# Prompt scores as two 128-row products with a stack of the keys' high and low halves, in place of a 128-row and a 64-row product

## The chip, the cores and the metric

The kernel runs on one core of one Trainium2 chip. It is one program: one launch reads the inputs from the chip's memory, does one decoder layer and writes all outputs. The metric is the device time of that launch in microseconds (us); lower is better. The figure for the kernel before is the median of three runs.

## The reference

One layer of a hybrid decoder is computed for a prompt of 1024 tokens and for 64 sampled tokens (8 sequences of 8), with a model width of 1024, in float32. Cut to what matters here:

```
mix:  h = rmsnorm(x) * (1 + scale1) + shift1
      ga, gc, xa, qb, kb, vb, qc, kc, vc = split(h @ w_in)
      A: short convolution of 256 channels
      B: 6 heads of width 64, three dilations, combined by their softmax denominators
      C: 6 query heads on 2 key/value heads, window 128, a learned sink for each head
      x = x + gate1 * (concat(A, B, C) @ w_out)
ffn:  x = x + gate2 * (silu(h2 @ w_gate) * (h2 @ w_up)) @ w_down
```

For the prompt's attention every head needs the scores `q . k / 8`, the softmax over the keys that its window (and, in group B, its dilations) allows, and the probabilities' sum of the values.

The products are to keep nearly float32 accuracy while TensorE runs them in float32r, a rounded form. So each operand x is split into two exact float32r halves, `hi = round(x)` and `lo = x - hi`, and `a . b` is taken as `hi.hi + hi.lo + lo.hi`; the product `lo.lo` is left out.

## The kernel before

**Stages.** Tokens lie along the free dimension, features on the 128 partitions. The program first computes the modulation and the first norm, then the input projection and the prompt's attention, then the sampled tokens' attention with the cached keys and values (with the output projection and the first feed-forward blocks of the prompt between its parts), then the feed-forward network. The large products are in `mm3` (L197): for each block of 128 contraction rows three matmuls, L202, L203 and L204, each with its own weights of 128 x 128 and 356 or 366 moving columns. The modulation of later stages is computed in between by `mod_tile` (L170), whose products at L178 use weights of only 32 columns.

**Order.** The code is written as a plain sequence. A scheduler puts each engine's instructions in order when the program is built, by its own estimate of times, and lets work of one stage fill gaps of another. Each engine then runs its list strictly in order and waits on semaphores.

**The prompt's attention** (L453 to L598) runs four times on a pair of heads' keys and values: once for the windowed group C, whose stack serves three query tiles, and three times for group B. The two heads of a block of 128 features lie on partitions 0 to 63 (`hd` = 0) and 64 to 127 (`hd` = 1); `o` is 64 * `hd`.

- `kv_stacks` (L459) prepares the keys. For each head, ScalarE writes the high half of the keys to `KH` on the head's own 64 partitions (L466); a transfer issued by GpSimd copies it to the other 64 partitions (L467); GpSimd subtracts to get the low half `KL`, on the head's own partitions (L468). L475 to L480 transpose the values.
- `attend` (L483) goes through heads and, in each, units of four (group C) or two (group B) blocks of 128 queries. For every two blocks it makes a query tile `QS` of 256 columns: ScalarE writes the high half on the head's 64 partitions (L496), GpSimd the low half on the other 64 (L497). The ring has three such tiles.
- The scores of one block of queries with up to 512 keys take two products into one tile `ps_s` of PSUM (two tiles in the ring). L517 contracts 128 rows, `[q_hi; q_lo] . [k_hi; k_hi]`. L518 contracts the head's 64 rows alone, `q_hi . k_lo`, and adds to it.
- VectorE adds the mask and takes the minimum (L524; the scores carry a minus sign), ScalarE takes the exponential and its sum (L532), VectorE the reciprocal (L534), VectorE or GpSimd the scaling (L535). TensorE transposes the probabilities (L560), ScalarE and VectorE split them (L563, L564), TensorE multiplies by the values (L569, weights of 128 x 128).

There are 48 query tiles (six calls of `attend`, eight tiles in each) and 120 pairs of L517 and L518: 12 pairs have 128 moving columns, 60 have 256, 18 have 384 and 30 have 512.

Of the kernel before, what the change touches and what calls it, by code (L numbers as in the profile page):

```python
# [8 lines left out]
F32 = mybir.dt.float32  # L9
F32R = mybir.dt.float32r  # L10
AF = mybir.ActivationFunctionType
OP = mybir.AluOpType
# [20 lines left out]
# buffers of the rings of tiles  # L33
# [6 lines left out]
# banks of the tags g, s, t, o in PSUM, and the tags that the early products take  # L40
# [4 lines left out]
# VectorE (v) or GpSimd (g) for each chunk; the chunks of the last norm that GpSimd scales  # L45
# [5 lines left out]
# tiles of the modulation after each projection, and gate blocks ahead of the sampled tokens'  # L51
# [12 lines left out]
def _build(nc, tc, d, cst, rows, actp, stream, psum):  # L64
# [18 lines left out]
    def halves(raw, sp=None):  # L83
        """The exact float32r halves of a float32 tile."""
# [35 lines left out]
    # constants  # L120
# [49 lines left out]
    def mod_tile(t, bank="g"):  # L170
        """256 columns of the modulation: a strip of 32 array columns for each quarter of the contraction."""
# [25 lines left out]
    def mm3(ps, sp, kcs, a, n, first=True, last=True):  # L197
        """ps[:, :n] (+)= W^T a for the K chunks, from exact halves of both operands."""
# [15 lines left out]
    def gemm(src, acts, gs, evac):  # L214
        """W^T a of one block of 128 features for the groups gs; src: the two halves of the block."""
# [10 lines left out]
    def inv_rms(pool, sums, n):  # L226
        """1 / sqrt(sums / D + EPS), one Newton step after the table's root."""
# [12 lines left out]
    # ---------------------------------------------------------------- first norm, h  # L240
# [3 lines left out]
    def early_split(b, i):  # L244
        """As split; the float32 tile stays for the product with the shift."""
        wraw[b, i] = load(d["w_in"][b, i], stp, "eraw", 4)
        return halves(wraw[b, i])
# [39 lines left out]
    # The input projection is W^T (x scale) / rms + W^T shift: the shifts are NB more columns of the third group,  # L287
    # except for the first two blocks.
# [21 lines left out]
    # ---------------------------------------------------------------- input projection  # L310
# [3 lines left out]
    def evac_norm(ps, g, r, s, b, scale=None):  # L314
        """The product over the rms of each token; b gets the bias, r the prompt's tokens and s the sampled ones."""
# [42 lines left out]
    def proj_plain(blk, name):  # L358
# [3 lines left out]
        if blk == 2:  # L362
            # the shifts come last
# [46 lines left out]
    def conv_steps(a):  # L410
# [8 lines left out]
        def times(ps, g, t, b, y, ys):  # L419
            """y and ys times the product of the group."""  # L420
# [32 lines left out]
    with tc.tile_pool(name="attn", bufs=1) as at:  # L453
# [4 lines left out]

        def kv_stacks(kn, vn):  # L459
            kr, vr = prow[kn], prow[vn]  # L460
            KH = []
            KL = at.tile([128, SEQ], F32R, tag="KL", bufs=1, name="KL")
            for hd in range(2):
                kh = at.tile([128, SEQ], F32R, tag="KH", bufs=2, name="KH")
                o = 64 * hd
                S.activation(kh[o:o + 64, :], kr[o:o + 64, :SEQ], AF.Copy)  # L466
                G.dma_start(kh[64 - o:128 - o, :], kh[o:o + 64, :])  # L467
                G.tensor_tensor(KL[o:o + 64, :], kr[o:o + 64, :SEQ], kh[o:o + 64, :].bitcast(F32),  # L468
                                op=OP.subtract)
                KH.append(kh)  # L470
# [10 lines left out]
            return KH, KL, Vt  # L481

        def attend(qn, stacks, mixrow, sinks=None):  # L483
            qr = prow[qn]
            KH, KL, Vt = stacks
            windowed = sinks is not None
            U = 4 if windowed else 2
            for hd in range(2):
                o = 64 * hd
                for j in range(8 // U):  # L490
                    P = []
                    for qi in range(U):
                        if qi % 2 == 0:
                            QS = at.tile([128, 256], F32R, tag="QS", bufs=3, name="QS")
                            qsrc = qr[o:o + 64, 128 * (U * j + qi):128 * (U * j + qi) + 256]
                            S.activation(QS[o:o + 64, :], qsrc, AF.Copy)  # L496
                            G.tensor_tensor(QS[64 - o:128 - o, :], qsrc, QS[o:o + 64, :].bitcast(F32),  # L497
                                            op=OP.subtract)
# [14 lines left out]
                        for si, (s0, sn) in enumerate(segs):  # L513
# [3 lines left out]
                            PE.matmul(ps[:, :sn], lhsT=QS[:, qsl], rhs=KH[hd][:, kk], start=True, stop=False)  # L517
                            PE.matmul(ps[:, :sn], lhsT=QS[o:o + 64, qsl], rhs=KL[o:o + 64, kk],  # L518
                                      start=False, stop=True)
# [585 lines left out]
```

## Time and profile before

| what | us |
|---|---|
| median of the three runs | 1460.31 |
| lowest and highest of them | 1457.1, 1461.98 |
| span of the profiled execution, first to last instruction | 1456.8 |
| TensorE matmul busy in it | 1422.3 |
| VectorE busy | 653.4 |
| ScalarE busy | 510.4 |
| GpSimd busy | 226.8 |

A row of the profile names the engine (PE is TensorE's matmuls, PEld its weight loads, DVE VectorE, ACT ScalarE, POOL GpSimd, SP the engine that issues most transfers), the line of the kernel, the tile written and those read, and the shape. On PE rows `128*128` or `64*128` is the part of the array in use, rows by columns; then come partitions x moving columns. A matmul's duration in the profile reaches from its start to its last result, and successive matmuls overlap; what one of them costs TensorE is the distance from its start to the start of the next, called its **pitch** below.

### The profile page before, as it was taken

The numbers are of one execution on the slowest core, as the hardware profiler recorded it, in microseconds if no ns is written. First come the engines' busy times: TensorE is split into PE (matmuls) and PEld (weight loads), VectorE is DVE, ScalarE is ACT, GpSimd is POOL, SyncE is SP. The second block draws the span as 40 slices with busy tenths as digits, with TensorE's granted clock in tenths as the row PEclk, the third lists the DMA queues.
The fourth block names the chain that finished last, engine by engine and source line by source line (L and its number), as shares of the span: only waits on it lengthen the run. The fifth ranks groups of instructions, "written<-read, shape, count | busy, mean of one in ns | idle before, by whom it ended". The sixth has DMA issues, their size and how long they took to land.

```text
span 1456.8 us, 23616 instructions
## 1 busy us (share of the span) xinstructions
PE 1422.3 (98%) x9289; PEld 1325.4 (91%) x9289; DVE 653.4 (45%) x1599; ACT 510.4 (35%) x1060; POOL 226.8 (16%) x288
## 2 busy tenths in 40 slices
PE   7999999999999999999999999999999999999996
PEld 5888888997787987978999999999999999999996
DVE  5456666536568324423564662233224321432145
ACT  5365654435555324322244412211221122112242
POOL 2142232313334321101110000000000000000014
PEclk9979999999999998999999999999999999999998
DMA  9252431244421779886434415641423242111103
GB/s 355 98 169 83 136 105 35 70 157 139 137 74 25 249 243 302 291 303 204 132 124 136 133 58 182 201 159 44 159 102 101 64 140 71 46 49 45 44 9 123
DMA packets 101439, 192.88 MB, mean 132 GB/s; under 512 B 14176, under 2 KB 51584, under 8 KB 100736
## 3 DMA queue, kind: packets, MB, share of 16 engines
q1 hardware_dynamic: 94112, 135.67, 29.0%
q10 hardware_dynamic: 6416, 53.55, 10.5%
q0 software_dynamic: 800, 2.14, 0.7%
q8 instruction: 73, 1.20, 0.3%
q14 instruction: 38, 0.31, 0.1%
HBM read 181.22 MB, written 59.23 MB: 165 GB/s over the span
## 4 chain that ended last, share of the span: by engine, by line
PE 92%; DMA 5%; issue 1%; DVE 1%; POOL 1%; SPq 0%; ACT 0%; POOLq 0%; ACTq 0%; DVEq 0%
PE ps_g L202 25%; PE ps_g L203 25%; PE ps_g L204 25%; PE ps_o L569 3%; PE ps_s L518 3%; PE ps_t L560 3%; DMA raw<-in_bv 2%; PE ps_s L517 2%; PE ps_g L178 1%; DMA wraw<-in_w_gu 1%; PE ps_s L651 1%; DMA raw<-in_bk 1%; PE ps_o L685 1%; DMA mraw<-in_wmod 1%; PE ps_g L185 0%
## 5 line engine op out<-in xcount | busy, mean ns | idle before, releaser
L202 PE MATMUL ps_g<-act,wsp 128*128 128x366 f32 (+1 forms) x1704 | 571.4, 336 | 4.2 <-DVE u L325 2.3
L203 PE MATMUL ps_g<-act,wsp 128*128 128x366 f32 (+1 forms) x1704 | 568.3, 334 | 0.5 <-DVE act L607 0.5
L204 PE MATMUL ps_g<-act,wsp 128*128 128x366 f32 (+1 forms) x1704 | 565.2, 333 | 0.4 <-POOL wsp L89 0.4
L202 PEld LDWEIGHTS ps_g<-act,wsp 128*128 128x128 f32 x1704 | 323.2, 190 | 17.5 <-issue 7.2
L203 PEld LDWEIGHTS ps_g<-act,wsp 128*128 128x128 f32 x1704 | 323.5, 190 | 8.0 <-issue 5.0
L204 PEld LDWEIGHTS ps_g<-act,wsp 128*128 128x128 f32 x1704 | 322.6, 189 | 5.1 <-issue 3.4
L88 ACT ACTIVATE wsp<-wraw 128x512 fp32r<-128x512 f32 x228 | 143.1, 630 | 472.7 <-PE ps_g L204 323.5
L89 DVE TENSOR_TENSOR wsp<-wraw,wsp 128x512 fp32r<-128x512 f32 x190 | 134.3, 707 | 353.7 <-ACT wsp L88 350.9
L204 PE MATMUL ps_g<-hid,wsp 128*128 128x366 f32 (+3 forms) x416 | 136.7, 329 | 0.0
L203 PE MATMUL ps_g<-hid,wsp 128*128 128x366 f32 (+3 forms) x416 | 136.1, 327 | 0.0
L202 PE MATMUL ps_g<-hid,wsp 128*128 128x366 f32 (+3 forms) x416 | 135.8, 328 | 0.2 <-DVE ts L757 0.2
L784 POOL TENSOR_TENSOR lacc<-lacc,tmp 128x416 f32<-128x416 f32 x9 | 9.8, 1084 | 637.8 <-ACT tmp L783 637.3
L202 PEld LDWEIGHTS ps_g<-hid,wsp 128*128 128x128 f32 x416 | 78.2, 188 | 0.5 <-PE ps_g L204 0.5
L203 PEld LDWEIGHTS ps_g<-hid,wsp 128*128 128x128 f32 x416 | 78.3, 188 | 0.0
L204 PEld LDWEIGHTS ps_g<-hid,wsp 128*128 128x128 f32 x416 | 78.2, 188 | 0.0
L89 POOL TENSOR_TENSOR wsp<-wraw,wsp 128x512 fp32r<-128x512 f32 x38 | 51.0, 1343 | 150.1 <-ACT wsp L88 149.9
L532 ACT ACTIVATE Sb<-Sb,st 128x257 f32<-128x257 f32 (+5 forms) x96 | 60.6, 632 | 25.4 <-DVE st L524 23.0
L564 DVE TENSOR_TENSOR PT<-ps_t,PT 128x512 fp32r<-128x512 f32 (+1 forms) x84 | 52.6, 637 | 21.3 <-ACT PT L563 20.8
L569 PE MATMUL ps_o<-PT,Vt 128*128 128x256 f32 (+1 forms) x348 | 60.4, 291 | 0.0
L753 DVE SCALAR_TENSOR_TENSOR p_qc<-ps_g,MOD,p_qc 128x366 f32<-128x366 f32 (+3 forms) x63 | 36.0, 573 | 49.5 <-PE ps_g L204 49.2
L569 PEld LDWEIGHTS ps_o<-PT,Vt 128*128 128x128 f32 x348 | 51.3, 195 | 5.6 <-issue 3.7
L563 ACT ACTIVATE PT<-ps_t 128x512 fp32r<-128x512 f32 (+1 forms) x84 | 44.7, 557 | 32.8 <-PE ps_t L560 26.0
(317 smaller groups left out, 1610.6 us busy)
## 6 DMA issues: line engine op xcount, KB each, us to landing
wraw<-in_w_gu SPq DMA_DIRECT2D x112, 256.0 KB, 2.6
wraw<-in_wmod SPq DMA_DIRECT2D x64, 256.0 KB, 4.0
raw<-in_bk SPq DMA_DIRECT2D x30, 512.0 KB, 7.5
raw<-in_bv SPq DMA_DIRECT2D x30, 512.0 KB, 8.8
wraw<-in_w_dn SPq DMA_DIRECT2D x48, 256.0 KB, 2.6
out_bk_b<-in_bk ACTq DMA_DIRECT2D x12, 1016.0 KB, 8.0
wraw<-in_w_in SPq DMA_DIRECT2D x36, 256.0 KB, 2.8
mraw<-in_wmod SPq DMA_DIRECT2D x32, 256.0 KB, 5.7
```

Source lines behind the costliest of these rows:

```text
L88: S.activation(sp[:, 0, :], raw, AF.Copy)
L89: (V if not state["sub"] or state["n"] % state["sub"] else G).tensor_tensor(sp[:, 1, :], raw, sp[:, 0, :].bitcast(F32), op=OP.subtract)
L202: PE.matmul(ps[:, :n], lhsT=w_hi, rhs=a(0, ak), start=first and j == 0, stop=False)
L203: PE.matmul(ps[:, :n], lhsT=w_hi, rhs=a(1, ak), start=False, stop=False)
L204: PE.matmul(ps[:, :n], lhsT=w_lo, rhs=a(0, ak), start=False, stop=last and j == m - 1)
L518: PE.matmul(ps[:, :sn], lhsT=QS[o:o + 64, qsl], rhs=KL[o:o + 64, kk], start=False, stop=True)
L532: S.activation(Sb[:, :ne], Sb[:, :ne], AF.Exp, scale=-1.0, bias=m, accum_out=st[:, 3:4])
L560: PE.transpose(pt[:, col:col + 128], Sb[:, (kb - k0) * 128:(kb - k0 + 1) * 128], ident)
L563: S.activation(PT[:, 0, :col], pt[:, :col], AF.Copy)
L564: V.tensor_tensor(PT[:, 1, :col], pt[:, :col], PT[:, 0, :col].bitcast(F32), op=OP.subtract)
L569: PE.matmul(po[:, q0:q0 + w], lhsT=Vt[:, kb, hd].rearrange("p a b -> p (a b)"), rhs=PT[:, hl, c0:c0 + w], start=fresh, stop=ch is chunks[- ...
L753: ins = V.scalar_tensor_tensor(x1[m][:, c0:c0 + k], ps[:, :k], MOD[:, gate + m, 0:1], x1[m][:, c0:c0 + k], op0=OP.mult, op1=OP.add)
```

## The change

The stack of keys of a head becomes one tile `KS`: the high half on the head's own 64 partitions, the low half on the other 64, written there by GpSimd's subtraction. The transfer that doubled the high half is gone, and so is `KL`. The queries get two tiles: `QH` with the high half on all 128 partitions (two ScalarE copies in place of one), and `QLO` with the low half on the head's 64 partitions and zeros on the others. The zeros are written once by four memsets, so the four `QLO` tiles are fixed ones, two for each head, used in turn; `QH` has a ring of three. The scores are now `[q_hi; q_hi] . [k_hi; k_lo]` and `[q_lo; 0] . [k_hi; k_lo]`, both with 128 rows. Every other edit of the diff drops a comment; lines behind the change move down by up to 7.

```diff
+        QL = [[at.tile([128, 256], F32R, name=f"QL{hd}{x}") for x in range(2)] for hd in range(2)]
+        for hd in range(2):
+            for ql in QL[hd]:
+                G.memset(ql[64 - 64 * hd:128 - 64 * hd, :].bitcast(F32), 0.0)
+        ql_n = [0, 0]
...
-            KH = []
-            KL = at.tile([128, SEQ], F32R, tag="KL", bufs=1, name="KL")
+            KS = []
             for hd in range(2):
-                kh = at.tile([128, SEQ], F32R, tag="KH", bufs=2, name="KH")
+                ks = at.tile([128, SEQ], F32R, tag="KS", bufs=2, name="KS")
                 o = 64 * hd
-                S.activation(kh[o:o + 64, :], kr[o:o + 64, :SEQ], AF.Copy)
-                G.dma_start(kh[64 - o:128 - o, :], kh[o:o + 64, :])
-                G.tensor_tensor(KL[o:o + 64, :], kr[o:o + 64, :SEQ], kh[o:o + 64, :].bitcast(F32),
+                S.activation(ks[o:o + 64, :], kr[o:o + 64, :SEQ], AF.Copy)
+                G.tensor_tensor(ks[64 - o:128 - o, :], kr[o:o + 64, :SEQ], ks[o:o + 64, :].bitcast(F32),
                                 op=OP.subtract)
...
-                            QS = at.tile([128, 256], F32R, tag="QS", bufs=3, name="QS")
+                            QH = at.tile([128, 256], F32R, tag="QH", bufs=3, name="QH")
+                            QLO = QL[hd][ql_n[hd] % 2]
+                            ql_n[hd] += 1
                             qsrc = qr[o:o + 64, 128 * (U * j + qi):128 * (U * j + qi) + 256]
-                            S.activation(QS[o:o + 64, :], qsrc, AF.Copy)
-                            G.tensor_tensor(QS[64 - o:128 - o, :], qsrc, QS[o:o + 64, :].bitcast(F32),
-                                            op=OP.subtract)
+                            S.activation(QH[o:o + 64, :], qsrc, AF.Copy)
+                            G.tensor_tensor(QLO[o:o + 64, :], qsrc, QH[o:o + 64, :].bitcast(F32), op=OP.subtract)
+                            S.activation(QH[64 - o:128 - o, :], qsrc, AF.Copy)
...
-                            PE.matmul(ps[:, :sn], lhsT=QS[:, qsl], rhs=KH[hd][:, kk], start=True, stop=False)
-                            PE.matmul(ps[:, :sn], lhsT=QS[o:o + 64, qsl], rhs=KL[o:o + 64, kk],
-                                      start=False, stop=True)
+                            PE.matmul(ps[:, :sn], lhsT=QH[:, qsl], rhs=KS[hd][:, kk], start=True, stop=False)
+                            PE.matmul(ps[:, :sn], lhsT=QLO[:, qsl], rhs=KS[hd][:, kk], start=False, stop=True)
```

**The order that the scheduler makes of it.** In the lists below a row is an instruction: line, operation, tile written `<-` tiles read, shape; the numbers on the names tell tiles apart. TensorE first, at the last query tile of the windowed group's first query block, where the scores stand in the projection of a later block (L202 to L204). Before:

```order
L517 MATMUL ps_s_1059<-KH_700,QS_1054 128x256
L518 MATMUL ps_s_1059<-KL_695,QS_1054 128x256
L202 MATMUL ps_g_1543<-act_123,wsp_1546 128x366
L517 MATMUL ps_s_1068<-KH_700,QS_1054 128x256
L518 MATMUL ps_s_1068<-KL_695,QS_1054 128x256
L203 MATMUL ps_g_1543<-act_123,wsp_1546 128x366
```

And of the change:

```order
L525 MATMUL ps_s_1072<-KS_706,QH_1066 128x256
L526 MATMUL ps_s_1072<-KS_706,QL11_694 128x256
L525 MATMUL ps_s_1081<-KS_706,QH_1066 128x256
L526 MATMUL ps_s_1081<-KS_706,QL11_694 128x256
L202 MATMUL ps_g_1564<-act_123,wsp_1567 128x366
L203 MATMUL ps_g_1564<-act_123,wsp_1567 128x366
```

The same products stand there with their partners (the second of a pair now reads the stack `KS` and a `QL` tile); the projection's product between the two pairs has moved behind them. In the whole list all 120 products of L518 stand among products of another shape, and only two of them are neighbours: 119 separate places. At ten of these the next product is one of L178. Blocks of products that use 32 columns of the array (L178 and those of the sampled tokens) number 71 before and 73 of the change, since L178 is cut into pieces at two more places. Behind the attention the lists are nearly the same.

TensorE again, at the first scores of all, just behind the projection of the second query block. Before:

```order
L178 MATMUL ps_g_1211<-wraw_1207,csil_104 32x256 x2
L517 MATMUL ps_s_821<-KH_696,QS_816 128x128
L518 MATMUL ps_s_821<-KL_695,QS_816 128x128
L517 MATMUL ps_s_830<-KH_696,QS_816 128x256
L518 MATMUL ps_s_830<-KL_695,QS_816 128x256
L517 MATMUL ps_s_843<-KH_696,QS_838 128x256
L518 MATMUL ps_s_843<-KL_695,QS_838 128x256
L178 MATMUL ps_g_1234<-wraw_1228,csil_104 32x256 x2
L178 MATMUL ps_g_1234<-wraw_1226,csil_104 32x256 x2
L517 MATMUL ps_s_852<-KH_696,QS_838 128x256
```

And of the change, from the same block of L178:

```order
L178 MATMUL ps_g_1224<-wraw_1222,csil_104 32x256 x2
L178 MATMUL ps_g_1224<-wraw_1220,csil_104 32x256 x2
L525 MATMUL ps_s_850<-KS_703,QH_844 128x256
L526 MATMUL ps_s_850<-KS_703,QL01_692 128x256
L525 MATMUL ps_s_859<-KS_703,QH_844 128x256
L526 MATMUL ps_s_859<-KS_703,QL01_692 128x256
L567 MATMUL ps_t_868<-ident_77,Sb_825 128x128 x2
L567 MATMUL ps_t_880<-ident_77,Sb_825 128x128
L525 MATMUL ps_s_900<-KS_703,QH_894 128x256
L526 MATMUL ps_s_900<-KS_703,QL00_691 128x256
```

The first two pairs have moved ahead of L178, into the end of the projection, and transposes of the first probabilities (L567, formerly L560) come before the second block of L178. As before, about a dozen pairs follow each other there with no projection's product between them.

GpSimd, where the first stack of keys is made. Before:

```order
L530 COPY Sb_819<-sinkB_93 128x1 x2
L467 DMA KH_696<-KH_696 64x1024
L468 TENSOR_TENSOR KL_695<-p_kc_567,KH_696 64x1024
L467 DMA KH_700<-KH_700 64x1024
L468 TENSOR_TENSOR KL_695<-p_kc_567,KH_700 64x1024
L497 TENSOR_TENSOR QS_816<-p_qc0_719,QS_816 64x256
```

And of the change:

```order
L464 MEMSET QL00_691 64x256
L464 MEMSET QL01_692 64x256
L464 MEMSET QL10_693 64x256
L464 MEMSET QL11_694 64x256
L537 COPY Sb_825<-sinkB_93 128x1 x2
L474 TENSOR_TENSOR KS_703<-p_kc_567,KS_703 64x1024
L474 TENSOR_TENSOR KS_706<-p_kc_567,KS_706 64x1024
L505 TENSOR_TENSOR QL00_691<-p_qc0_724,QH_821 64x256
```

The four memsets stand ahead, the two transfers are gone, the subtractions stay. ScalarE's list grows by 48 copies of 64 x 256 (L506), each near the one of L504 that was L496. SP's list differs in one place: the writing of one block of values (`out_bv_p`) stands one weight load later.

More of the change, by code (lines that the diff above doesn't have):

```diff
@@ L457, in _build @@
         SP.dma_start(maskC, d["maskC"])
+        QL = [[at.tile([128, 256], F32R, name=f"QL{hd}{x}") for x in range(2)] for hd in range(2)]
[3 more added lines that the diff above has]
+        ql_n = [0, 0]
         def kv_stacks(kn, vn):
             kr, vr = prow[kn], prow[vn]
-            KH = []
-            KL = at.tile([128, SEQ], F32R, tag="KL", bufs=1, name="KL")
+            KS = []
             for hd in range(2):
-                kh = at.tile([128, SEQ], F32R, tag="KH", bufs=2, name="KH")
+                ks = at.tile([128, SEQ], F32R, tag="KS", bufs=2, name="KS")
                 o = 64 * hd
-                S.activation(kh[o:o + 64, :], kr[o:o + 64, :SEQ], AF.Copy)
-                G.dma_start(kh[64 - o:128 - o, :], kh[o:o + 64, :])
-                G.tensor_tensor(KL[o:o + 64, :], kr[o:o + 64, :SEQ], kh[o:o + 64, :].bitcast(F32),
+                S.activation(ks[o:o + 64, :], kr[o:o + 64, :SEQ], AF.Copy)
+                G.tensor_tensor(ks[64 - o:128 - o, :], kr[o:o + 64, :SEQ], ks[o:o + 64, :].bitcast(F32),
                                 op=OP.subtract)
-                KH.append(kh)
+                KS.append(ks)
             Vt = at.tile([128, 8, 2, 2, 64], F32R, tag="V", bufs=1, name="Vt")
@@ L480, in kv_stacks @@
                                 Vt[:, q * 4:q * 4 + 4, :, 0, :].bitcast(F32), op=OP.subtract)
-            return KH, KL, Vt
+            return KS, Vt
         def attend(qn, stacks, mixrow, sinks=None):
             qr = prow[qn]
-            KH, KL, Vt = stacks
+            KS, Vt = stacks
             windowed = sinks is not None
```

## The prediction

> **What bounds the kernel now.** I read the page first: busy times, the clock's slices, the chain that ended last.
>
> ```profile
> span 1456.8 us, 23616 instructions
> PE 1422.3 (98%) x9289; PEld 1325.4 (91%) x9289; DVE 653.4 (45%) x1599; ACT 510.4 (35%) x1060; POOL 226.8 (16%) x288
> ...
> PEclk9979999999999998999999999999999999999998
> ...
> PE 92%; DMA 5%; issue 1%; DVE 1%; POOL 1%; SPq 0%; ACT 0%; POOLq 0%; ACTq 0%; DVEq 0%
> ```
>
> TensorE is busy for nearly the whole span, and 92% of the chain is its own work. So what TensorE spends is what the kernel takes, unless a stage has another limit. The edit lies in the prompt's attention, from about 75 to 460 us; I read that stage as one window.
>
> ```profile
> 75.00:460.00 385.00, 384.27 (x2296) 326.92 (x2295) 232.46 (x675) 204.02 (x476) 128.88 (x151) 0.97 0.33 105
> ```
>
> The columns of the row are start and end, the length, then the busy us of PE, PEld, DVE, ACT and POOL, the clock granted, and the DMA share. TensorE stands idle for 0.7 us in 385 (385.00 less 384.27); VectorE is busy for 60%, ScalarE for 53%, GpSimd for 33%. So in this stage too each us that TensorE saves is a us of the kernel, as long as the others keep up.
>
> Busy does not mean useful, though. The next question is the pitch of the two score products, read from the timeline of PE (start, duration) around a pair that stands alone between large products:
>
> ```profile
> 166.90 0.33 PE L204 MATMUL ps_g<-act,wsp 128*128 128x366 f32 x1
> 167.07 0.33 PE L202 MATMUL ps_g<-act,wsp 128*128 128x366 f32 x1
> 167.24 0.28 PE L569 MATMUL ps_o<-PT,Vt 128*128 128x256 f32 x1
> 167.35 0.33 PE L203 MATMUL ps_g<-act,wsp 128*128 128x366 f32 x1
> 167.52 0.33 PE L204 MATMUL ps_g<-act,wsp 128*128 128x366 f32 x1
> 167.69 0.28 PE L517 MATMUL ps_s<-KH,QS 128*128 128x256 f32 x1
> 167.89 0.38 PE L518 MATMUL ps_s<-KL,QS 64*128 64x256 f32 x1
> 168.20 0.43 PE L202 MATMUL ps_g<-act,wsp 128*128 128x366 f32 x1
> 168.47 0.33 PE L203 MATMUL ps_g<-act,wsp 128*128 128x366 f32 x1
> 168.64 0.63 PE L569 MATMUL ps_o<-PT,Vt 128*128 128x256 f32 x4
> 169.10 0.27 PE L560 MATMUL ps_t<-ident,Sb 128*128 128x128 f32 x1
> ```
>
> A large product has a pitch of 0.17 us (166.90 to 167.07), one of 256 columns on the whole array 0.115 us (the four from 168.64 to 169.10; 167.24 to 167.35 agrees). L517 before L518 takes 0.20, L518 itself 0.31, and the L202 behind it 0.27. From 167.52 to 168.47 stand L204, L517, L518 and L202, in 0.95 us; at the pitches of the whole array they would take 0.17 + 0.115 + 0.115 + 0.17 = 0.57. **So one visit of the 64-row shape costs 0.38 us more** than the same columns at the whole shape. It falls in three places: 0.085 before L518 starts, 0.195 in it, 0.10 in the product behind it.
>
> The Trainium skill, "TensorEngine Tiling (Array Packing)", Key Properties, says that a change of tiling mode drains TensorE. The rows agree that a change costs; but a drain alone, at the 0.085 us before L518, twice for a visit, would make 0.17 us of the 0.38, and the saving below about 19 us instead of 42. I take the rows.
>
> **The change part by part.**
>
> *The 64-row products go.* PEld shows how many there are:
>
> ```profile
> L518 PEld LDWEIGHTS ps_s<-KL,QS 64*128 64x128 f32 x120 | 22.6, 189 | 22.5 <-issue 18.0
> ```
>
> All 120 become products of 128*128. The order list has them at 119 separate places, and 119 x 0.38 = 45.2 us. Four corrections follow.
>
> First, the twelve with 128 columns cost less:
>
> ```profile
> 159.83 0.33 PE L202 MATMUL ps_g<-act,wsp 128*128 128x366 f32 x1
> 159.99 0.22 PE L517 MATMUL ps_s<-KH,QS 128*128 128x128 f32 x1
> 160.15 0.33 PE L518 MATMUL ps_s<-KL,QS 64*128 64x128 f32 x1
> 160.40 0.43 PE L203 MATMUL ps_g<-act,wsp 128*128 128x366 f32 x1
> 160.67 0.33 PE L204 MATMUL ps_g<-act,wsp 128*128 128x366 f32 x1
> ...
> 161.78 1.06 PE L560 MATMUL ps_t<-ident,Sb 128*128 128x128 f32 x8
> 162.59 0.36 PE L517 MATMUL ps_s<-KH,QS 128*128 128x256 f32 x1
> ```
>
> From 159.83 to 160.67 is 0.84; eight dense products of 128 columns take 0.81, so 0.10 each, and the four would take 0.17 + 0.10 + 0.10 + 0.17 = 0.54. That is 0.30 instead of 0.38: 12 x 0.08 = 1.0 us less. Second, at ten places the neighbour behind is L178, which uses 32 columns; there a change of shape stays, and I leave half a visit, 10 x 0.19 = 1.9 us less. Third, the new order cuts L178 at two more places: 0.8 us less, taking a visit of that shape for as dear. Fourth, some visits lie in a stretch at half clock, where they cost more. Its timeline, then two windows: of L518 alone (length, busy PE and PEld, clock, DMA), and of all engines over the run of scores that it falls in:
>
> ```profile
> 89.26 0.64 PE L178 MATMUL ps_g<-wraw,csil 128*32 128x256 f32 x8 [0.55 <-DMA wraw<-in_wmod]
> ...
> 92.55 0.58 PE L518 MATMUL ps_s<-KL,QS 64*128 64x256 f32 x1
> 93.06 0.58 PE L517 MATMUL ps_s<-KH,QS 128*128 128x256 f32 x1
> 93.57 0.58 PE L518 MATMUL ps_s<-KL,QS 64*128 64x256 f32 x1
> ...
> 100.24 1.22 PE L569 MATMUL ps_o<-PT,Vt 128*128 128x256 f32 x4
> 101.26 0.63 PE L560 MATMUL ps_t<-ident,Sb 128*128 128x128 f32 x2
> ```
>
> ```profile
> 91.00:108.10 17.10, 4.10 (x8) 2.00 (x7) 0.50 0.43 147
> 87.00:104.70 17.70, 5.22 (x11) 2.63 (x11) 0.61 0.60 206
> ```
>
> ```profile
> 87.00:104.70 17.70, 17.15 (x69) 12.07 (x69) 10.28 (x46) 11.80 (x34) 6.37 (x12) 0.61 0.60 206
> ```
>
> A pair takes 1.02 there (92.55 to 93.57), two dense products 2 x 1.02/4 = 0.51; the difference is 0.51 instead of 0.38. The first window counts eight, one of them at its edge: 7 x 0.13 = 0.9 us more. The sum is 45.2 - 1.0 - 1.9 - 0.8 + 0.9 = 42.4, in round numbers **42 us** of TensorE's time.
>
> *The weights of the second product* are loaded for 128 rows instead of 64. The PEld row above has 189 ns for one of 64 rows; that of L517, with 128 rows, is
>
> ```profile
> L517 PEld LDWEIGHTS ps_s<-KH,QS 128*128 128x128 f32 x120 | 23.7, 197 | 7.1 <-issue 4.5 <-DVE st L524 0.8 <-DVE Sb L535 0.4
> ```
>
> so the rows cost nothing, and between products of one shape the load lies under the product before, as for L569.
>
> *ScalarE, GpSimd and the transfer.* Three groups by line, a row of GpSimd's timeline, and the transfer's row (size, us to landing):
>
> ```profile
> L496 ACT ACTIVATE QS<-p_q 64x256 fp32r<-64x256 f32 x24 | 9.8, 413 | 13.7 <-PE ps_s L518 13.5
> ...
> L497 POOL TENSOR_TENSOR QS<-p_q,QS 64x256 fp32r<-64x256 f32 x24 | 18.5, 772 | 54.7 <-ACT QS L496 54.3
> ...
> L467 POOL DMA_DIRECT2D KH<-KH x8 | 4.4, 546 | 8.8 <-ACT KH L466 8.8
> ```
>
> ```profile
> 76.46 0.55 POOL L467 DMA_DIRECT2D KH<-KH  x1 [3.85 <-ACT KH L466]
> ```
>
> ```profile
> KH<-KH POOLq DMA_DIRECT2D x8, 256.0 KB, 4.3
> ```
>
> ScalarE gets 48 more copies of 0.41 us, 19.8 us. They lie beside TensorE's work: ScalarE would be busy for 204 + 20 = 224 us of a stage of about 343, or 65%, VectorE for 68%. If that cover were gone, all of them would cost 20 us. GpSimd loses eight issues, 4.4 us, and eight transfers that land after 4.3 us; no row shows TensorE waiting for them, so I count 0, and a gain of a few us if the first scores now come earlier has no place to show while the projection fills TensorE. Four memsets of 64x256 are not in this trace; between 0 and the subtraction's 0.77 us each, that is at most 3.1 us. GpSimd idles 3.85 us just there, ahead of 76.46, so they cost 0. A query tile's first product now waits for two copies on ScalarE, 0.83 us, instead of 0.41 + 0.77 = 1.18; the second waits for GpSimd as before.
>
> SP's one exchange moves a write of a result behind one weight load; nothing on chip reads it.
>
> *What is late next.* The weak place is the first run of scores, from 87 to 104.7 us, where no projection fills TensorE. Eleven visits go (the window of L518), some 5 us, so TensorE alone would need 12.7 of the 17.7 us. But ScalarE is busy for 11.8 us there (window row above) and gets six or so more copies, 2.5 us: 14.3 us. So at least 1.6 us of the 5 are not had; as these chains go through VectorE and ScalarE in turn, I take 3. Elsewhere TensorE waits for 0.7 us now, and I add 1. **The new waits: 4 us.** The lower bound is 0. For the upper one, let each of the 36 units of attention (12 windowed, 24 dilated) show one exponential that is hidden now:
>
> ```profile
> L532 ACT ACTIVATE Sb<-Sb,st 128x257 f32<-128x257 f32 (+5 forms) x96 | 60.6, 632 | 25.4 <-DVE st L524 23.0
> ```
>
> 36 x 0.63 = 23 us. I choose 4, near the stage's own 0.7, since windows leave a third of each helper's time free.
>
> **The sum.** The profiled execution would go from 1456.8 by -42 + 4 to 1418.8. The median of the runs is 1460.3, 3.5 above that span, which I keep: **1422 us**.
>
> **The rivals.**
>
> *A: the clock too.* The granted clock is half from about 91 to 108 us (the 7 in the third slice of PEclk's row, 0.50 in the window of L518). That took 17 us at half speed, so some 8.5 us of TensorE's time. It follows a stretch of dear visits and a hole of 0.55 us. With whole shapes the array is fed better, and if the half clock doesn't come, and the waits are 0, the time is 1460 - 42 - 8.5 = 1410. Against it: the hole before 89.26 waits for a transfer, which won't come sooner, and the chains of that run leave holes of their own. The Trainium skill, "TensorE: Matmul & The Clock Gate", Part 1, says that the clock is halved by how busy the array was in a window of about 3.4 us; the half clock behind such a stretch agrees. The chance: 0.17.
>
> *B: the helpers set the pace.* The scores come faster than VectorE's minimum and ScalarE's exponential can follow in many units, and the 23 us of the bound come due, or half of them with an extra stretch of half clock (another 17 us cost 8.5). Time: 1460 - 42 + 12 to 23, so 1430 to 1441. For it: after the change VectorE and ScalarE are both near two thirds. Against: projection products stand between most units. The chance: 0.17.
>
> *C: nothing goes.* The dear pitch isn't the shape's but belongs to the pair's tile in PSUM or to the split operands. Then L526 costs what L518 does, and the time stays at 1459 to 1460. Against it: L517 and L569 write and read the same kinds of tiles at a whole pitch when no other shape is beside them, and L178, whose shape differs too, is as dear at its edges. The chance: 0.04.
>
> *D: slower, by the ring of the low halves.* Each head has two QLO tiles in fixed turns, where three QS tiles served both. GpSimd's subtraction for a tile must wait until TensorE is through with the last but one of that head; if TensorE then has nothing else, it idles for the subtraction and a queued copy, 0.77 + 0.41 = 1.18 us, at each of the 48 tiles: 57 us, so 1460 - 42 + 57 = 1475. It decides from 42/48 = 0.88 us a tile. For it: ScalarE waits already for a ring of three (the 13.5 us in its row). Against: TensorE does not wait for any of that now, and a tile is needed only each 385/48 = 8 us. The chance: 0.03.
>
> **How the numbers follow.** My forecast, 1415 to 1430, has 0.59; A 0.17, B 0.17, C 0.04, D 0.03. The range leaves out C and D and a little of the rest: low is A with 3 us for the rounding of 0.38 (119 x 0.025), 1407; high is B's end, 1441. A measurement of this kernel tells about 0.3%, 4 us, from no change. Forecast, A and B are faster by more than that: 0.93. C is within it: 0.04. D is slower: 0.03.
>
> **What would show it.** In the changed kernel's timeline, L525 and L526 should each have the pitch of L569 (0.12 for 256 columns) with a plain 0.17 behind them. The attention should end about 38 us sooner, and all behind it keep its length. TensorE's waits in the stage should be some 4 us, most of them before 105 us. The prediction is wrong if L526 keeps 0.31 (C), if PE waits for Sb, st or PT of the helpers add to over 10 us (B), or for QLO (D); and the clock's third slice tells A.

## The result, and the profile after

| what | us |
|---|---|
| kernel before, median of 4 runs (lowest to highest) | 1461.14 (1457.1 to 1464.26) |
| changed kernel, median of 4 runs (lowest to highest) | 1425.82 (1422.57 to 1429.4) |
| ratio, with its 95% interval | 0.9757 [0.973, 0.9785] |
| span of the profiled execution (its time: 1429.4) | 1427.6 |

The change saves 35 us. The forecast was 1422, its range 1407 to 1441. The profiled execution is the slowest of the four, and its mean granted clock is 0.983, as in the profile before; the spans of these two, 1456.8 and 1427.6 us, are 29 us apart. The page of the changed kernel, in the places that were read before:

```profile
span 1427.6 us, 23603 instructions
...
PE 1383.2 (97%) x9289; PEld 1319.7 (92%) x9289; DVE 650.8 (46%) x1599; ACT 529.3 (37%) x1108; POOL 222.7 (16%) x284
...
PEclk9999999999999998999999999999999999999998
...
PE 88%; DMA 6%; DVE 2%; issue 2%; ACT 1%; POOL 1%; SPq 0%; ACTq 0%; POOLq 0%; DVEq 0%
```

TensorE has the same 9289 products and is busy for 39 us less; that is where the gain comes from, and 10 of the 39 come back as idle time (34.5 us of the span before, 44.4 now). Its share of the chain falls from 92% to 88%: other engines are waited for now. ScalarE's 48 new copies show as 19 us more of busy time, and the dip to 7 in the clock's third slice is gone.

The timeline of PE of the changed kernel (start, duration) shows two pairs of scores between large products:

```profile
105.75 0.33 PE L204 MATMUL ps_g<-act,wsp 128*128 128x366 f32 x1
105.92 0.28 PE L525 MATMUL ps_s<-KS,QH 128*128 128x256 f32 x1
106.04 0.28 PE L526 MATMUL ps_s<-KS,QL 128*128 128x256 f32 x1
106.16 0.28 PE L525 MATMUL ps_s<-KS,QH 128*128 128x256 f32 x1
106.27 0.28 PE L526 MATMUL ps_s<-KS,QL 128*128 128x256 f32 x1
106.39 0.33 PE L202 MATMUL ps_g<-act,wsp 128*128 128x366 f32 x1
106.56 0.32 PE L203 MATMUL ps_g<-act,wsp 128*128 128x366 f32 x1
```

Each score product now has a pitch of 0.12 us (105.92, 106.04, 106.16, 106.27, 106.39), and the large product behind has a plain 0.17. The row of L526's weight loads, from the groups by line of PEld, tells the same of all 120:

```profile
L526 PEld LDWEIGHTS ps_s<-KS,QL 128*128 128x128 f32 x120 | 23.3, 194 | 0.2
```

A load takes 194 ns (189 before, with half the rows), and the idle time ahead of the loads is 0.2 us where it was 22.5.

What that is worth in the stage is read from one window of PE for each kernel, from 75 us to the last value product of the attention (start and end, length, PE's busy time, products, clock, DMA share). First before, then after:

```profile
75.00:482.40 407.40, 403.86 (x2413) 0.97 0.34 108
```

```profile
75.00:447.10 372.10, 362.26 (x2412) 0.98 0.34 112
```

The work is the same to a product, so the lengths can be compared: 35.3 us less. TensorE is busy for 41.6 us less, and its idle time (length less busy) grows from 3.5 to 9.8 us: 6.3 of the 41.6 are given back as waits. The whole span is only 29.2 us shorter (1456.8 to 1427.6), so another 6 are lost behind the attention in this execution.

The waits of PE between 75 and 430 us in the changed kernel (who waited, for whom, us in all, times, longest), the three largest:

```profile
PE ps_t L567 <- DVE Sb L542: 5.3, 3, 2.4
PE ps_g L178 <- DMA wraw<-in_wmod: 0.9, 1, 0.9
PE ps_s L525 <- ACT PT L570: 0.4, 1, 0.4
```

Three waits for VectorE's scaling of the probabilities, L542, make most of it. Two of them, 1.74 and 2.44 us, stand beside the same GpSimd operation. Here is the longer one, in the timelines of DVE, POOL and PE:

```profile
319.36 2.93 DVE L542 TENSOR_SCALAR Sb<-Sb,st 128x1024 f32<-128x1024 f32 x1
```

```profile
319.39 2.34 POOL L474 TENSOR_TENSOR KS<-p_k,KS 64x1024 fp32r<-64x1024 f32 x1
```

```profile
322.34 0.33 PE L567 MATMUL ps_t<-ident,Sb 128*128 128x128 f32 x1 [2.44 <-DVE Sb L542]
```

GpSimd's subtraction for the keys' low half lasts from 319.39 to 321.73. VectorE's scaling starts 0.03 us ahead of it and needs 2.93 us. TensorE, which transposes what the scaling writes, idles for 2.44. At 182 us it is a scaling of 256 columns, beside the same GpSimd operation:

```profile
182.32 1.77 DVE L542 TENSOR_SCALAR Sb<-Sb,st 128x256 f32<-128x256 f32 x1
```

```profile
181.59 2.35 POOL L474 TENSOR_TENSOR KS<-p_k,KS 64x1024 fp32r<-64x1024 f32 x1 [6.62 <-ACT KS L473]
```

It ends at 184.09, just behind GpSimd at 183.94. For comparison the groups of both sizes in the kernel before (count, then busy us and mean ns):

```profile
L535 DVE TENSOR_SCALAR Sb<-Sb,st 128x256 f32<-128x256 f32 x48 | 19.7, 421 | 0.9
L535 DVE TENSOR_SCALAR Sb<-Sb,st 128x1024 f32<-128x1024 f32 x6 | 6.4, 1068 | 0.1
```

VectorE looks as if it were held until GpSimd is nearly through. The kernel before has one such case too, in DVE's timeline, beside a subtraction of GpSimd from 381.83 to 384.21; no PE row waits for it:

```profile
382.11 2.65 DVE L535 TENSOR_SCALAR Sb<-Sb,st 128x1024 f32<-128x1024 f32 x1
```

So the change did not bring the hold; its new order put it where TensorE has nothing else to do. The Trainium skill, "SBUF — State Buffer", SBUF: two separate sides, says that VectorE and GpSimd share one pair of ports under an exclusive lock: a GpSimd operation and a VectorE operation that uses both of its ports, or has two inputs in SBUF, exclude each other, and whichever starts first holds the pair for its whole instruction. The durations agree with a lock. The order does not: in the longer case the scaling, which was held, had begun 0.03 us ahead by the records. The profile does not show which ports the scaling used. An experiment below moves the subtraction away.

### The profile page after: what moved, and what is told of

Read it like the earlier page. It is cut to its first block, busy times and chain, and to the rows that moved or that the text cites. A ratio compares the mean times of both kernels' runs of the same rounds, so it can differ in the third digit from the quotient of the medians.

```text
span 1427.6 us, 23603 instructions
## 1 busy us (share of the span) xinstructions
PE 1383.2 (97%) x9289; PEld 1319.7 (92%) x9289; DVE 650.8 (46%) x1599; ACT 529.3 (37%) x1108; POOL 222.7 (16%) x284
## 4 chain that ended last, share of the span: by engine, by line
PE 88%; DMA 6%; DVE 2%; issue 2%; ACT 1%; POOL 1%; SPq 0%; ACTq 0%; POOLq 0%; DVEq 0%
PE ps_g L202 25%; PE ps_g L203 25%; PE ps_g L204 25%; PE ps_o L576 3%; PE ps_t L567 2%; DMA raw<-in_bv 2%; PE ps_s L525 1%; PE ps_g L178 1%; DMA wraw<-in_w_gu 1%; PE ps_s L526 1%; DMA raw<-in_bk 1%; DMA mraw<-in_wmod 1%; PE ps_s L658 1%; PE ps_o L692 1%; DMA wraw<-in_wmod 0%
## 5 line engine op out<-in xcount | busy, mean ns | idle before, releaser
L202 PE MATMUL ps_g<-act,wsp 128*128 128x366 f32 (+1 forms) x1704 | 568.4, 334 | 5.0 <-ACT wsp L88 2.6
L204 PE MATMUL ps_g<-act,wsp 128*128 128x366 f32 (+1 forms) x1704 | 564.3, 332 | 0.4 <-POOL wsp L89 0.4
L202 PEld LDWEIGHTS ps_g<-act,wsp 128*128 128x128 f32 x1704 | 323.6, 190 | 12.5 <-issue 5.5
L204 PEld LDWEIGHTS ps_g<-act,wsp 128*128 128x128 f32 x1704 | 322.9, 190 | 4.7 <-issue 3.3
L204 PE MATMUL ps_g<-hid,wsp 128*128 128x366 f32 (+3 forms) x416 | 136.5, 328 | 0.0
L202 PE MATMUL ps_g<-hid,wsp 128*128 128x366 f32 (+3 forms) x416 | 135.6, 328 | 0.2 <-DVE ts L764 0.2
L202 PEld LDWEIGHTS ps_g<-hid,wsp 128*128 128x128 f32 x416 | 78.1, 188 | 0.5 <-PE ps_g L204 0.5
L204 PEld LDWEIGHTS ps_g<-hid,wsp 128*128 128x128 f32 x416 | 78.2, 188 | 0.0
L567 PE MATMUL ps_t<-ident,Sb 128*128 128x128 f32 x306 | 51.9, 283 | 5.9 <-DVE Sb L542 5.3
```

The lines of the kernel that those rows point to most:

```text
L202: PE.matmul(ps[:, :n], lhsT=w_hi, rhs=a(0, ak), start=first and j == 0, stop=False)
L204: PE.matmul(ps[:, :n], lhsT=w_lo, rhs=a(0, ak), start=False, stop=last and j == m - 1)
L567: PE.transpose(pt[:, col:col + 128], Sb[:, (kb - k0) * 128:(kb - k0 + 1) * 128], ident)
```

## The experiments

Every run is compared with the kernel before on the same chip, as a ratio with its 95% interval. The medians of before were 1461.63 us for the first four experiments (64 rows in the changed kernel, 128 rows in the kernel before, the copy, three products), 1459.16 for the next four, and 1459.43 for the last four.

The runs also differ in their clock, which matters for differences of a few us. Each execution has a mean granted clock, recorded to 0.001. At half clock work takes twice as long: four value products last 1.22 us at 100.24 and 0.63 at 168.64, in the prediction's rows. So (1 - clock) x time is an estimate of what an execution lost to the clock. It is an upper one, since nothing is lost where TensorE waits anyway: among executions of the same kernel the time moves by about 0.7 us for each us of it. Its mean over the executions of each kernel:

| kernel | lost to the clock, us |
|---|---|
| before, in the three groups | 26.4, 24.2, 23.6 |
| the change, at first and once more | 21.7, 19.6 |
| the change with 64 rows again | 24.6 |
| shape alone | 18.1 |
| transfer replaced by a copy | 21.9 |
| three 64-row products | 31.5 |
| shape alone, more copies | 19.9 |
| the change, keys on VectorE | 16.7 |
| the change, one tile of low halves | 24.3 |
| the change, modulation's order | 19.1 |
| the three combinations | 25.4, 25.3, 24.2 |

Whether an edit or chance brought a kernel its clock is not shown; but a difference that is no larger than that of these figures can't be credited to the edited work.

### The shape alone, undone in the changed kernel

Only the second product's operands are cut to the head's 64 partitions; copies, memsets, stack and fixed tiles stay.

```diff
-PE.matmul(ps[:, :sn], lhsT=QLO[:, qsl], rhs=KS[hd][:, kk], start=False, stop=True)
+PE.matmul(ps[:, :sn], lhsT=QLO[o:o + 64, qsl], rhs=KS[hd][o:o + 64, kk], start=False, stop=True)
```

> The changed kernel with one edit: its second product contracts the head's own 64 rows alone (the others are zeros), so the result is the same. Shape theory: the 64-row product is back at 119 places, each costs 0.38 us as before, so the time goes from 1426 back up by 40 to 43 us, to 1462 to 1470. Rival (the gain came from the stack, the missing transfer and the earlier start): it stays at 1422 to 1430.

Measured: 1465.6 us, ratio 1.0029 [1.0013, 1.0045]. The whole gain goes, 40 us from 1425.82, and the dear pitch is back, with 0.21 us before the 64-row product and 0.31 in it, in the timeline of PE:

```profile
176.26 0.28 PE L525 MATMUL ps_s<-KS,QH 128*128 128x256 f32 x1
176.47 0.38 PE L526 MATMUL ps_s<-KS,QL 64*128 64x256 f32 x1
176.78 0.33 PE L525 MATMUL ps_s<-KS,QH 128*128 128x128 f32 x1
```

So the shape makes the gain, and neither the stack nor the missing transfer does. At equal shapes the rest of the change costs 4 us (0.29% of 1461.63; the interval is 1.9 to 6.6), or about 6 with the clock set aside (24.6 lost instead of 26.4).

### The shape alone, changed in the kernel before

```diff
-PE.matmul(ps[:, :sn], lhsT=QS[o:o + 64, qsl], rhs=KL[o:o + 64, kk],
+PE.matmul(ps[:, :sn], lhsT=QS[:, qsl], rhs=KL[:, kk],
           start=False, stop=True)
```

> The kernel before with one edit: the second product runs over all 128 rows of the query tile and of KL, so the other head's low halves times this one's are added, which the reference doesn't have (a term of the size of low times low). The transfer, the key tiles and the query tiles stay. Shape theory: 42 us of TensorE's time go, less 4 to 7 of new waits: 1419 to 1428. Rival (stack and transfer): 1457 to 1463.

Measured: 1416.34 us, ratio 0.9691 [0.9677, 0.9706]; 45 us faster than before, and 3 below the low end expected. Of the 45 up to 8 go with the clock (18.1 us lost instead of 26.4), which leaves 37. One edit to one product, though it adds a term of low times low that the reference does not have, gives more than the whole change does. Its timeline of PE has the pitch of the changed kernel:

```profile
101.57 0.28 PE L517 MATMUL ps_s<-KH,QS 128*128 128x256 f32 x1
101.69 0.28 PE L518 MATMUL ps_s<-KL,QS 128*128 128x256 f32 x1
101.81 0.28 PE L517 MATMUL ps_s<-KH,QS 128*128 128x256 f32 x1
101.93 0.28 PE L518 MATMUL ps_s<-KL,QS 128*128 128x256 f32 x1
102.04 0.33 PE L202 MATMUL ps_g<-act,wsp 128*128 128x366 f32 x1
```

And its window to the last value product is 11.3 us shorter than that of the changed kernel, with as much work:

```profile
75.00:435.80 360.80, 355.48 (x2408) 0.99 0.39 121
```

Idle are 5.3 us (9.8 in the changed kernel), so 4.5 of the 11.3 are waits, and the rest is a shorter busy time at a somewhat higher clock: the clock is half for 10 us of this window, and for 17 of the changed kernel's.

### The transfer replaced by a copy, in the kernel before

```diff
-G.dma_start(kh[64 - o:128 - o, :], kh[o:o + 64, :])
+S.activation(kh[64 - o:128 - o, :], kr[o:o + 64, :SEQ], AF.Copy)
```

> The kernel before with the transfer that doubles the keys' high halves replaced by a second copy on ScalarE; shapes stay. Shape theory: no change, 1457 to 1465. Rival (the transfer was part of the gain): up to 35 us less, 1426 to 1450.

Measured: 1459.73 us, ratio 0.9987 [0.9978, 0.9996]. That is 2 us less, by the interval 0.6 to 3.2; but 4.5 us less went to the clock (21.9 instead of 26.4), so it is not shown that the transfer itself costs more than the copy in its place. Counting its removal at nothing was close either way.

### Three 64-row products: is the price one of a visit or of a product?

The first product is split into two with 64 rows, one for each half of the queries, so that three products of that shape stand together; the transfer goes. Not shown are the lines that give the queries' low half its own tile `QLW`, on the head's own rows, and both heads one tile of high key halves.

```diff
...
-PE.matmul(ps[:, :sn], lhsT=QS[:, qsl], rhs=KH[hd][:, kk], start=True, stop=False)
+PE.matmul(ps[:, :sn], lhsT=QS[o:o + 64, qsl], rhs=KH[hd][o:o + 64, kk],
+          start=True, stop=False)
+PE.matmul(ps[:, :sn], lhsT=QLW[o:o + 64, qsl], rhs=KH[hd][o:o + 64, kk],
+          start=False, stop=False)
 PE.matmul(ps[:, :sn], lhsT=QS[o:o + 64, qsl], rhs=KL[o:o + 64, kk],
           start=False, stop=True)
```

> The kernel before with three products of 64 rows for each piece of scores (high.high, low.high, high.low on the head's own rows), no transfer. 360 products of 64 rows in 116 visits of that shape. If the cost belongs to the visit (one change in, one out): the visits stay as dear and 120 more products cost their columns, some 0.155 us each, 19 us: 1474 to 1484. If the cost belongs to each product of 64 rows (0.38 each): 240 more of them, some 91 us on top of the 19: 1550 to 1580.

Measured: 1485.11 us, ratio 1.0159 [1.0134, 1.0184], 1 us above the range of a price per visit (of the 23 us more than before, 5 may be the clock's: 31.5 us lost instead of 26.4), and far from a price per product. The timeline of PE shows where a visit pays:

```profile
128.39 0.32 PE L203 MATMUL ps_g<-act,wsp 128*128 128x366 f32 x1
128.65 0.38 PE L518 MATMUL ps_s<-KH,QS 64*128 64x256 f32 x1
128.87 0.28 PE L520 MATMUL ps_s<-KH,QLW 64*128 64x256 f32 x1
128.99 0.28 PE L522 MATMUL ps_s<-KL,QS 64*128 64x256 f32 x1
129.19 0.44 PE L204 MATMUL ps_g<-act,wsp 128*128 128x366 f32 x1
129.47 0.33 PE L202 MATMUL ps_g<-act,wsp 128*128 128x366 f32 x1
```

Inside the visit a 64-row product of 256 columns has the pitch of a whole one (128.87 to 128.99). The dear intervals are those next to the change of shape: 0.26 instead of 0.17 ahead, 0.22 instead of 0.12 in the first, 0.20 in the last, and 0.28 instead of 0.17 behind.

### More copies in the kernel with the shape alone

The second experiment with one more ScalarE copy for each query tile, 48 in all, overwritten at once by GpSimd's subtraction; it asks whether the copies explain what the change gives away.

```diff
...
 S.activation(QS[o:o + 64, :], qsrc, AF.Copy)
+S.activation(QS[64 - o:128 - o, :], qsrc, AF.Copy)
```

> The kernel before with the second product on 128 rows (1416), and in each of the 48 query tiles one more ScalarE copy of 64 x 256 into the half that GpSimd then overwrites: the 48 copies of the change without its stack and its low tiles. If ScalarE's 20 us are what the change gives back of the shape's gain: 1423 to 1428. If they lie beside other work: 1415 to 1419.

Measured: 1420.92 us, ratio 0.9735 [0.9718, 0.9752], between the two expectations. It lies 4.6 us above 1416.34, but with another order of the program, which has five more visits of the 32-column shape (76 instead of 71); at 0.38 each these could be 1.9 of them, and 1.8 more went to the clock (19.9 instead of 18.1). The copies cost little, and the run doesn't settle how little.

### The keys' low half on VectorE

In the changed kernel, so that GpSimd's 2.3 us operations beside the attention go.

```diff
-G.tensor_tensor(ks[64 - o:128 - o, :], kr[o:o + 64, :SEQ], ks[o:o + 64, :].bitcast(F32),
+V.tensor_tensor(ks[64 - o:128 - o, :], kr[o:o + 64, :SEQ], ks[o:o + 64, :].bitcast(F32),
                 op=OP.subtract)
```

> The changed kernel with the subtraction that makes the keys' low half on VectorE in place of GpSimd. If GpSimd's 2.35 us instruction holds VectorE's scaling at the two places where TensorE then waited 1.7 and 2.4 us, no scaling of 256 columns takes over 1.4 us any more, TensorE's waits for it fall from 5.3 us to under 2, and the time falls by 3 to 4 us; the list has eight more visits of 32-column products (81 for 73), some 3 us back: 1421 to 1427. If VectorE was late for another reason: its waits stay, 1427 to 1432.

Measured: 1421.18 us, ratio 0.9732 [0.9714, 0.9749]. VectorE's timeline has the subtraction, and a scaling of 1024 columns at its usual length:

```profile
314.04 1.22 DVE L474 TENSOR_TENSOR KS<-p_k,KS 64x1024 fp32r<-64x1024 f32 x1
...
315.95 1.15 DVE L542 TENSOR_SCALAR Sb<-Sb,st 128x1024 f32<-128x1024 f32 x1
```

All six scalings of 1024 columns together have a mean of 0.82 us (1.21 in the changed kernel):

```profile
L542 DVE TENSOR_SCALAR Sb<-Sb,st 128x1024 f32<-128x1024 f32 x6 | 4.9, 818 | 0.2
```

PE has no wait for L542 left among those from 75 to 430 us; the largest are now

```profile
PE ps_g L202 <- DVE u L325: 1.8, 1, 1.8
PE ps_g L178 <- DMA wraw<-in_wmod: 0.9, 1, 0.9
PE ps_s L525 <- ACT Sb L539: 0.8, 1, 0.8
```

So the long scalings were VectorE held by GpSimd: without that operation there are none, and their 5.3 us of waits go, of which another wait takes back 1.8. The kernel is 4.6 us faster than the change in its first comparison and 2.5 faster than in its second (below), whose interval it overlaps; but it lost 5.0 and 2.9 us less to the clock (16.7 instead of 21.7 and 19.6). So the hold is shown, and that its waits go; what they are worth in the kernel's time is not.

### One tile of low halves for each head

```diff
-QLO = QL[hd][ql_n[hd] % 2]
+QLO = QL[hd][0]
```

> The changed kernel with one tile of low halves for each head in place of two. If the ring of the low halves costs time already at two (the rival of the prediction that ends slower), one doubles its waits: 1436 to 1480. If the ring is covered by other work, one costs little: 1423 to 1433.

Measured: 1431.51 us, ratio 0.9807 [0.9781, 0.9833]. PE's waits from 75 to 430 us have none for QL:

```profile
PE ps_g L178 <- DMA wraw<-in_wmod: 4.5, 1, 4.5
PE ps_o L576 <- ACT PT L570: 2.9, 1, 2.9
PE ps_t L567 <- DVE Sb L542: 2.6, 2, 1.4
```

With half the tiles the kernel takes 6 to 8 us more than the change, of which up to 2.6 to 4.7 can be the clock (24.3 us lost instead of 21.7 and 19.6). What the rest is, is not shown. The ring does hold GpSimd, whose subtraction waits 64.7 us in all for L526, in 27 turns, but TensorE has other work meanwhile: the 57 us of rival D do not come even with one tile.

### One visit in place of two, in the modulation's products

The eight products of L178, which use 32 columns of the array, are ordered as one run by a single condition, their two halves in reverse.

```diff
-for hf in range(2):
-    first = None
+first = None
+for hf in (1, 0):
...
-                    start=(hf == 0), stop=(hf == 1))
+                    start=(hf == 1), stop=(hf == 0))
```

> The changed kernel with the eight products of a modulation tile ordered so that the first needs the weights that land last: 58 visits of 32-column products in place of 73. If such a visit costs as much as one of 64 rows, 15 x 0.38 = 5.7 us go: 1418 to 1422. If it costs nothing, or the later start makes TensorE wait for the weights: 1425 to 1435.

Measured: 1415.46 us, ratio 0.9698 [0.9679, 0.9716]. It has 58 visits of the 32-column shape instead of 73; at 0.38 each that is 5.7 us, and 8 to 10 came, of which the clock can have given 0.5 to 2.6; so something beyond the visits seems to have helped. This is the fastest of the kernels that compute the same three terms as the kernel before, faster than both kernels compared here.

### The change again, and three combinations

In one group on one chip: the changed kernel once more; the two edits that helped it, together; the shape alone with the modulation's order; and that with the keys' subtraction on VectorE as well.

> The changed kernel once more, beside the three variants of this group: 1422 to 1430.

> The changed kernel with both edits: the keys' low half by VectorE, and the modulation's eight products behind their last weights (68 visits of 32 columns; 73 in the change, 58 with the second edit alone). If the two gains are separate: 1415 less 4, some 1411. If the visits decide: ten more than with the second edit alone cost 3.8 us, and 1415 to 1419 comes out.

> The kernel before with the second product on 128 rows (its extra term of low times low of the other head) and the modulation's products behind their last weights: 70 visits for 71. If visits decide, no gain over 1416: 1414 to 1418. If the later start itself helps: under 1412.

> As the one before (128 rows, extra term, modulation's products behind their last weights), with the keys' low half by VectorE: 66 visits. 1411 to 1416 if visits and the held VectorE both count; 1416 or more if neither does in this layout.

| kernel | median us | ratio to before |
|---|---|---|
| the change again | 1423.68 | 0.9761 [0.9733, 0.979] |
| the change, modulation's order and keys on VectorE | 1428.42 | 0.9789 [0.9762, 0.9816] |
| shape alone, modulation's order | 1427.97 | 0.9782 [0.9761, 0.9804] |
| the same, keys on VectorE too | 1425.31 | 0.9757 [0.9724, 0.9789] |

The change repeats. The three combinations miss: the gains of 8 and of 3 to 5 us do not add, and the modulation's order, which helped the changed kernel, costs 12 us (1427.97 less 1416.34) in the kernel with the shape alone. In all the kernels with that order TensorE is idle and at a lower clock early, ahead of the attention. The windows from 30 to 50 us (length, busy PE, PEld, DVE, ACT and POOL, clock, DMA) of the change, and of the change with both edits:

```profile
30.00:50.00 20.00, 20.00 (x128) 18.14 (x126) 13.44 (x33) 12.71 (x26) 6.76 (x4) 1.00 0.65 212
```

```profile
30.00:50.00 20.00, 16.31 (x89) 15.66 (x87) 16.70 (x25) 10.13 (x19) 8.19 (x4) 0.83 0.61 209
```

128 products start there in the one and 89 in the other. The kernel with the modulation's order alone has this too and is the fastest all the same, so it doesn't explain the misses by itself. Over the whole span the misses go with the clock in part: the first two lost 25.4 and 25.3 us to it, where the kernels that they were to improve lost 19.1 and 18.1. That can be 6 to 7 of the 12 to 13 us by which they are slower than these. What makes the rest, and what lowered the clock, was not found.

## Why the prediction was right

**The 42 us of the 64-row visits were close.** Undoing the shape alone takes 40 to 42 us, making it alone gives 45. With the clock set aside both are about 37 (40 less 2.9, 45 less 8.3), with the new waits in them; the forecast had 42 less 4, 38. In the windows up to the last value product TensorE's busy time falls by 41.6 us with the change and by 48.4 with the shape alone; the half clock there lasts 24 us before, 17 and 10 after, so 3.5 and 7 of these are the clock's, and some 38 and 41 are left for the 42. The attention ended 35.3 us sooner, instead of the 38 forecast. That the price belongs to a change of shape and not to a product, on which the count of 119 rested, is shown by the three products in one visit. The drain alone of the Trainium skill's "TensorEngine Tiling (Array Packing)", Key Properties, which at the 0.085 us of the rows would have made 19 us, is too small by about half: the intervals in and behind the visit belong to the price.

**The dense pitch** came as read from other products: 0.12 and a plain 0.17. Rival C is out, and the loads of 128 rows cost nothing, as said.

**The terms set at nothing together cost 4 us**, by the first experiment, and about 6 with the clock set aside: copies, memsets, transfer, fixed tiles and the order that comes of them. This is a term mis-sized by 0.3 to 0.4% of the time. Which of them it is stays open.

**The waits were mis-sized and put in the wrong place.** The prediction gave 4 us, most of them before 105 us. Over the attention TensorE idles 6.3 us more than before, and in the first run of scores only a part of them: the window from 87 to 104.7 us, of the changed kernel,

```profile
87.00:104.70 17.70, 15.64 (x96) 12.31 (x89) 13.26 (x56) 17.18 (x51) 8.10 (x18) 0.81 0.56 200
```

is idle for 2.06 us (17.70 less 15.64) where it was 0.55. ScalarE is busy for 17.18 of the 17.70 us, so the suspicion that it would be late next was good, but the stretch costs 1.5. The larger part lies at 182 and 320 us, where GpSimd's subtraction holds VectorE: a step that the prediction did not have, since it took GpSimd's operations for work beside others, though a row of the trace of before showed a hold.

**Rival A came in part.** In the window above the clock is 0.81 instead of 0.61, which is 17.70 x 0.20 = 3.5 us more of the array. In the second profile of the same changed kernel the half clock is absent there altogether:

```profile
87.00:104.70 17.70, 15.81 (x106) 13.01 (x107) 16.53 (x66) 17.01 (x49) 8.18 (x18) 1.00 0.61 206
```

The dips move between executions, so one execution tells little: in the profiled pair the mean clock of the whole span is the same, 0.983, and the gain there is 29 us. Over all executions the change lost 21.7 and 19.6 us to the clock, before 23.6 to 26.4. In the group that has both, up to 4 of the 35.8 us came by the clock. The forecast had left the clock as it was, so part of its nearness is luck: the work alone gave some 29 to 32 us, 6 to 9 fewer than the 38 forecast, and a higher clock made up for over half of what was missing.

**"All behind it keeps its length" was wrong by some 6 us** in the profiled execution. Between the same two points in the stage of the sampled tokens, the windows of before and after are

```profile
625.10:683.60 58.50, 53.24 (x476) 46.08 (x472) 12.88 (x29) 15.38 (x27) 7.74 (x7) 0.97 0.84 287
```

```profile
589.70:653.60 63.90, 56.21 (x480) 48.77 (x476) 12.86 (x28) 16.01 (x28) 6.57 (x6) 0.92 0.76 261
```

That is 5.4 us more for the same work: 3.0 of busy time, at a clock of 0.92 instead of 0.97, and 2.4 of idle time. TensorE waits there longer for a cached value's transfer, among others; first before, then after:

```profile
PE ps_o L685 <- DMA raw<-in_bv: 2.1, 1, 2.1
```

```profile
PE ps_o L692 <- DMA raw<-in_bv: 3.6, 1, 3.6
```

Why that transfer is later against the work was not tried.

**Rivals B and D** did not come. PE's waits for Sb, st and PT add to 6.0 us, below the 10 that were to show B, and the longest of them are a held VectorE, not the minimum and the exponential setting the pace; no row has PE waiting for QL. What remains open is why the shape alone, in the kernel before, is 7 to 9.5 us faster than the change. The clock can be 1.5 to 3.6 of it, and the held VectorE and the copies may be some, but no run shows how much; and the combinations show that such parts do not add, as each edit also gives the program another order.

## What to carry to other kernels

A product that uses part of the array's rows costs by its edges, when its neighbours use the whole of it: look at the pitch of the product and of the one behind it, not at its own length, and count the places where the shape changes. Filling the rows with zeros, or with a term small enough to keep, cost TensorE nothing here: both products had the pitch of the whole array. Once TensorE is the bound, edits of helper work that are worth a few us reorder the program and move the time by as much again; each needs its own run, and their gains are not to be added. Before a few us are credited to an edit, compare the mean granted clocks of the executions.

## What was not expected of the hardware

- VectorE's scaling of 128x1024 took 2.93 us, where the kernel before has a mean of 1.07 for six, one held case of 2.65 among them, and one of 128x256 1.77 instead of 0.42, while GpSimd subtracted 64x1024; with that subtraction on VectorE, where it takes 1.22 us instead of GpSimd's 2.34, no scaling was longer than 1.43.
- A product of 64 rows between others of 64 rows has the pitch of a whole one, 0.12 us for 256 columns; all of the 0.38 us of a visit lies at its edges.
- In one stretch of 17.7 us the same program ran at a granted clock of 0.81 in one execution and of 1.00 in another.
